# A decoder layer in split precision: another tile for the second input, sums of weight pairs issued one by one, up weights split in one piece

## The chip, the cores and the metric

One core of a Trainium2 chip. The time is that of one execution on the device in microseconds, the median of several runs. TensorE (PE) multiplies, VectorE (DVE), ScalarE (ACT) and GpSimd (POOL) do the rest, SyncE (SP) issues nearly all transfers. Each engine works through its own instructions in the order in which the program holds them.

## The reference, cut to what matters

One layer of a decoder trunk for 256 tokens of width 1024, in float32. `p` is the second input, 256 wide per token.

```python
proj = x @ w_in[i]                       # queries, keys, values of three mixers
o_a, o_b, o_c = dsa_mixer(...), dilated_mixer(...), moba_mixer(...)
gates = sigmoid(x @ w_gate[i])           # three per channel
merged = gates_0 * (o_a @ w_br_a) + gates_1 * (o_b @ w_br_b) + gates_2 * (o_c @ w_br_c)
x = layer_norm(ALPHA * x + merged @ w_out[i], ...)
h = square(relu(x @ w_up[i])) @ w_down[i]                  # 1024 -> 4096 -> 1024
ple = sigmoid(x @ w_ple_gate[i]) * (p[i] @ w_ple[i])
x = layer_norm(ALPHA * x + h + ple, ...)
```

All mixers add a bias that depends on the distance of query and key.

## The kernel before

**Split operands.** A float32 product is made of three products of rounded operands: `prod` (L180 to L189) multiplies the high and low halves as high x high, high x low and low x high. The high half of a weight is a rounded copy by ScalarE (L109 or L111), the low half the rest, a subtraction by VectorE (L118 or L122), in the first stages partly by GpSimd. The class `Weights` does that for one *unit* of 128 x 1024 weights at a time: SP loads it into one of five `raw` tiles (L102), and it is split into one of five pairs of tiles `whi` and `wlo`. `get(u)` splits up to unit u+4, so splits run some units ahead of the matmuls. The places of the unit's eight blocks of 128 columns within the tile are given by `at`. If they don't stand at one distance, `Apart.runs` cuts the work into several instructions. Up units (L639) have `UP = (16, *range(192, 1088, 128)), (64, *range(208, 1104, 128))`: the first block stands apart, so that ScalarE and VectorE each do two blocks (256 columns) and then six (768).

**Order.** The code is written in program order, and a scheduler with a timeline of its own sets each engine's order; `tc.issue_after(x)` holds an instruction until after `x` in it, `tc.keep_in_program_order` pins it.

**Stages.** First the projections, the three mixers, and between their steps the gates ("g") and merges ("c", "a"), which fill TensorE. The bias of a head lies in a tile `T` of the pool `tp`, tag "T", three buffers: `toeplitz` (L263 to L269) loads three heads' rows with three transfers (L265). The dilated mixer (`slots`, L456) keeps its exponentials in tiles `eb` of the pool `wk2`, two buffers. The second input is loaded at L582 and L583 into a tile `pr` that takes one of these two `eb` places, and is split at L584 (ScalarE) and L585 (VectorE) into `ph` and `pl`, which are used 120 us later.

Then the output product, the first norm, the gate of `p`, and the **up projection**: 32 blocks `f` of 128 features, each 8 matmuls of 512 columns with the high half of the weights (L932) and 8 of 256 with the low half (L935), then relu and square. Its tile of moving operands is `x1`.

**The down stage** multiplies the 32 blocks with rows of `w_down`. Part of them go in *pairs* (a tuple in `SEQ`, L860) by Strassen's scheme, seven products in place of eight: four units per pair, 21 matmuls, in place of two units with 12 each. A single block is one unit, 12 matmuls of 512 columns.

```python
wr[i] = r = xr[:, i % 2] if i else ...      # load(i), L880: the pair's two weight blocks
dve.tensor_tensor(t[:, 0:1024], r[:, 512:1536], r[:, 0:1024], op=ALU.subtract)      # L894
dve.tensor_tensor(r[:, 512:1024], r[:, 1024:1536], t[:, 0:512], op=ALU.subtract)    # L895
dve.tensor_tensor(t[:, 1024:1536], r[:, 1536:2048], r[:, 512:1024], op=ALU.subtract)  # L896
```

`form(i)` (L889) makes these three differences; the pair's four units are the second loaded row, the first difference, the first row after the second difference, and the third difference (512 wide). `xr` has two places. It takes the place of `x1`, so that its first loads wait for the up projection's last matmul. When the last unit of pair i is split (`last_part`), i+2 is put on the list `later`, and `weights` (L978) then calls `load(i+2)` and `form(i+2)` at once. A load waits until the splits of pair i have read the place, and VectorE's differences wait for the load. Pairs 1 and 2 are loaded and formed after the up projection (L964 to L966), pair 0 within it.

Of the kernel before, what the change touches and what calls it, by code (L numbers as in the profile page):

```python
# [11 lines left out]
F32 = mybir.dt.float32  # L12
# [130 lines left out]
def hybrid_layer(ctx: ExitStack, tc: tile.TileContext, x0, xn, pT, wqk, wva, wvb, wg, wbc, wba,  # L143
# [423 lines left out]
    for j in range(2):  # L567
# [13 lines left out]
        fill("g")  # L581
    pr = wk2.tile([128, 2, S], F32, name="pr", tag="eb")  # L582
    nc.sync.dma_start(pr, pT)  # L583
# [54 lines left out]
    u_pg = [add(wpg[i], 1024) for i in range(8)]  # L638
    UP = (16, *range(192, 1088, 128)), (64, *range(208, 1104, 128))  # L639
    u_up = [[add(wup[i], 1024, at=UP)] for i in range(32)]  # L640

# [210 lines left out]
    for b in range(2):  # L852
        for c in range(2):
# [5 lines left out]

    SEQ = ((0, 1), 2, 3, (4, 5), 6, 7, (8, 9), 10, (11, 12), 13, (14, 15), 16, (17, 18), 19,  # L860
           (20, 21), 22, 23, 24, 25)
# [27 lines left out]
    def form(i):  # L889

        t = p3.tile([128, 2, D], F32, name="rows", tag="rows") if i % 2 else Y
        wt[i] = t = t.rearrange("p b d -> p (b d)")
        r = wr[i].rearrange("p b d -> p (b d)")
        dve.tensor_tensor(t[:, 0:1024], r[:, 512:1536], r[:, 0:1024], op=ALU.subtract)  # L894
        dve.tensor_tensor(r[:, 512:1024], r[:, 1024:1536], t[:, 0:512], op=ALU.subtract)  # L895
        dve.tensor_tensor(t[:, 1024:1536], r[:, 1536:2048], r[:, 512:1024], op=ALU.subtract)  # L896

    def last_part(i):
        r = wt[i][:, 1024:1536]
        if 0 < i < len(PAIRS) - 2:  # L900
            later.append(i + 2)
        return r

    later = []
    u_dn = {}
    for k in (*SEQ, *LATE):
        if k in PAIRS:
            i = PAIRS.index(k)
            u_dn[k] = [add(f, n) for f, n in (
                (lambda i=i: wr[i][:, 1], 1024), (lambda i=i: wt[i][:, 0:1024], 1024),  # L910
                (lambda i=i: wr[i][:, 0], 1024), (lambda i=i: last_part(i), 512))]
        elif k < 30:
            u_dn[k] = [add(wdn[k], 1024)]

    def relu2(dst, ps):
# [6 lines left out]
    for f in range(32):  # L922
        if f == 16:
            with tc.issue_after(W.loads[-1]):
                load(0)
            with tc.issue_after(W.subs[-1]):
                form(0)
        ps = mmbank(512).rearrange("p (a t b) -> p a t b", a=2, b=2)
# [35 lines left out]
    for i in (1, 2):  # L964
        load(i)
        form(i)  # L966

# [9 lines left out]

    def weights(u):  # L978
        w = W.get(u)
        while later:  # L980
            i = later.pop(0)
            load(i)
            form(i)
        return w
# [191 lines left out]
```

## Time and profile before

| | |
|---|---|
| median of 3 runs | 417.64 us (417.42 to 418.87) |
| profiled execution | 417.59 us, of which 415.8 us are the span that the trace shows |
| mean granted TensorE clock | 0.996 |
| TensorE, VectorE, ScalarE, GpSimd busy | 404.6, 348.3, 277.4, 121.6 us |
| in the chain that ended last | PE 79%, DVE 9%, DMA 6% of the span |

Busy times of engines overlap, so they don't add up. A busy TensorE isn't one at full rate: matmuls are pipelined, the trace's ends of them are modelled, and the time from one start to the next tells the rate. An idle engine costs something only where TensorE waits for it, directly or through others.

### The profile page before, as it was taken

Reading aid. Unit: us, or ns where it says so; the run is one execution under the profiler, and the core shown is the slowest. Engines: PE = TensorE matmul, PEld = TensorE weight load, DVE = VectorE, ACT = ScalarE, POOL = GpSimd, SP = SyncE. Lnnn points to the kernel's source line nnn. Section 1 sums busy time; section 2 is a strip of 40 time slices with the busy share of each in tenths; the row PEclk is TensorE's granted clock in tenths of the full one; section 3 lists DMA queues with packets and bytes.
Section 4 is the critical chain, followed back from the end, with each engine's and each line's share of the span. In section 5 each row is a group of like instructions: output and inputs, shape, how many; then the busy total and the mean of one; then the engine's idle time right before and its main releaser. Section 6 shows DMA issues by size and latency. Waiting matters only on the chain.

```text
span 415.8 us, 7826 instructions
## 1 busy us (share of the span) xinstructions
PE 404.6 (97%) x2804; PEld 374.1 (90%) x2804; DVE 348.3 (84%) x650; ACT 277.4 (67%) x530; POOL 121.6 (29%) x128
## 2 busy tenths in 40 slices
PE   8999999999999999999999999999999999899993
PEld 7989999999999999999887889999999888688882
DVE  4868769897777789889978889999999797999856
ACT  5787476495798786867515668887889675558310
POOL 1579456175353657500000002433330000000001
PEclk9999999999999999999999999999999999999998
DMA  8796766567474408477981677695675377546502
GB/s 283 291 338 184 273 166 199 170 202 259 143 208 135 134 18 285 123 217 259 332 314 36 225 268 207 223 298 177 195 214 186 128 271 215 189 159 212 192 2 102
DMA packets 27964, 83.49 MB, mean 201 GB/s; under 512 B 3184, under 2 KB 6792, under 8 KB 27540
## 3 DMA queue, kind: packets, MB, share of 16 engines
q1 hardware_dynamic: 27360, 81.51, 60.3%
q10 hardware_dynamic: 468, 1.41, 0.9%
q8 instruction: 22, 0.36, 0.4%
q14 instruction: 18, 0.15, 0.1%
q0 software_dynamic: 96, 0.06, 0.0%
HBM read 81.88 MB, written 1.09 MB: 200 GB/s over the span
## 4 chain that ended last, share of the span: by engine, by line
PE 79%; DVE 9%; DMA 6%; ACT 2%; issue 2%; SPq 0%; POOL 0%; DVEq 0%; ACTq 0%
PE mm L188 34%; PE b L188 17%; PE mm L932 13%; PE mm L935 7%; DMA xr<-in_wdn_dram 3%; PE b L370 3%; DVE wlo L118 3%; PE b L522 2%; DVE wlo L122 2%; DMA G<-in_x_dram 1%; DMA pr<-in_pT_dram 1%; PE b L412 1%; ACT whi L111 1%; PE b L419 1%; DVE Y L894 1%
## 5 line engine op out<-in xcount | busy, mean ns | idle before, releaser
L111 ACT CAST whi<-raw 128x1024 fp32r<-128x1024 f32 (+3 forms) x92 | 89.5, 986 | 35.6 <-PE b L188 14.5
L122 DVE TENSOR_TENSOR wlo<-raw,whi 128x256 fp32r<-128x256 f32 (+3 forms) x118 | 94.7, 826 | 15.3 <-ACT whi L111 11.4
L188 PE MATMUL mm<-xh,whi 128*128 128x256 f32 x336 | 89.1, 278 | 0.0
L122 POOL TENSOR_TENSOR wlo<-raw,whi 128x384 fp32r<-128x384 f32 (+1 forms) x50 | 68.7, 1383 | 65.0 <-ACT whi L111 57.6
L188 PE MATMUL mm<-xl,whi 128*128 128x256 f32 x336 | 87.1, 277 | 0.0
L188 PE MATMUL mm<-xh,wlo 128*128 128x256 f32 x336 | 79.4, 278 | 0.0
L188 PEld LDWEIGHTS mm<-xh,whi 128*128 128x128 f32 x336 | 64.5, 192 | 0.9
L188 PEld LDWEIGHTS mm<-xl,whi 128*128 128x128 f32 x336 | 64.5, 192 | 0.2
L932 PE MATMUL mm<-x,whi 128*128 128x512 f32 x256 | 60.8, 380 | 0.0
L188 PEld LDWEIGHTS mm<-xh,wlo 128*128 128x128 f32 x336 | 58.7, 192 | 0.2
L188 PE MATMUL b<-whi,store 128*128 128x512 f32 x168 | 52.5, 380 | 0.3 <-DVE b L1006 0.3
L932 PEld LDWEIGHTS mm<-x,whi 128*128 128x128 f32 x256 | 46.1, 190 | 5.1
L118 DVE TENSOR_TENSOR wlo<-raw,whi 128x1024 fp32r<-128x1024 f32 (+2 forms) x38 | 43.2, 1156 | 3.5 <-ACT whi L111 3.4
L749 POOL TENSOR_TENSOR rs<-rs,half 128x1 f32<-128x1 f32 x4 | 2.7, 666 | 142.5 <-DVE rs L748 142.5
L109 ACT CAST whi<-raw 128x256 fp32r<-128x256 f32 x64 | 36.4, 613 | 6.1 <-PE b L188 3.7
L188 PEld LDWEIGHTS b<-whi,store 128*128 128x128 f32 x168 | 31.8, 189 | 4.9 <-DVE b L1006 0.7
L935 PEld LDWEIGHTS mm<-x,wlo 128*128 128x128 f32 x256 | 33.6, 191 | 1.7
L935 PE MATMUL mm<-x,wlo 128*128 128x256 f32 x256 | 33.8, 275 | 0.0
L188 PE MATMUL b<-wlo,store 128*128 128x512 f32 x84 | 32.1, 382 | 0.6 <-DVE wlo L118 0.6
L956 POOL TENSOR_TENSOR a<-a 128x128 f32<-128x128 f32 x7 | 7.3, 1042 | 57.3 <-ACT a L918 51.7
L188 PE MATMUL mm<-op,whi 128*128 128x256 f32 x128 | 22.1, 278 | 0.0
L188 PE MATMUL b<-whi,x 128*128 128x512 f32 x64 | 19.8, 384 | 0.1
(221 smaller groups left out, 818.9 us busy)
## 6 DMA issues: line engine op xcount, KB each, us to landing
raw<-in_wup_dram SPq DMA_DIRECT2D x32, 512.0 KB, 4.4
raw<-in_wg_dram SPq DMA_DIRECT2D x24, 512.0 KB, 4.6
raw<-in_wqk_dram SPq DMA_DIRECT2D x18, 512.0 KB, 5.0
raw<-in_wdn_dram SPq DMA_DIRECT2D x18, 512.0 KB, 4.3
raw<-in_wout_dram SPq DMA_DIRECT2D x8, 512.0 KB, 4.5
raw<-in_wpg_dram SPq DMA_DIRECT2D x8, 512.0 KB, 5.2
T<-tabd SPq DMA_DIRECT2D x24, 128.0 KB, 4.0
xr<-in_wdn_dram SPq DMA_DIRECT2D x6, 512.0 KB, 3.6
```

Of the source, the lines that this page charges most:

```text
L109: i = nc.scalar.copy(blocks(hi, a, b), blocks(r, a, b))
L111: i = nc.scalar.copy(hi, r)
L118: i = e.tensor_tensor(lo[:, x], r[:, x], hi[:, x].bitcast(F32), op=ALU.subtract)
L122: i = e.tensor_tensor(blocks(lo, *x), blocks(r, *x), blocks(hi, *x).bitcast(F32), op=ALU.subtract)
L188: i = pe.matmul(ps, lhsT=a[x], rhs=b[y], start=first and n == 0, stop=last and n == 2, skip_group_check=more)
L370: m = pe.matmul(ss[2 * n + h][:, QC[b]], lhsT=q[d, x, c], rhs=k[d, y, 0:128 * (b + 1)], start=i == 0, stop=i == 2)
L412: pe.transpose(t[:, 128 * i:128 * i + 128], P[:, 128 * i:128 * i + 128], ident)
L419: pe.matmul(v[:, 256 * i:].rearrange("p (m c q) -> p m c q", c=64, q=2), lhsT=V[:, i, vh], rhs=pt[:, b0:b1].rearrange("p b a (q c) -> p (b ...
L522: pe.matmul(pairs(first[f]), lhsT=w[:, k, 128 * f:128 * f + 128], rhs=inturn(x[:, k]), start=k == i == 0, stop=k == KT - 1 and i == 2)
L932: pe.matmul(ps, lhsT=hi[:, c], rhs=x1[:, :, k].rearrange("p b a t -> p a t b"), start=k == 0, stop=False)
L935: pe.matmul(ps[:, 0], lhsT=lo[:, c], rhs=x1[:, :, k, 0].rearrange("p b t -> p t b"), start=False, stop=k == KT - 1)
L956: pool.tensor_tensor(sums[2], a11, a21, op=ALU.subtract)
```

## The change

Four edits:

1. `pr` is a tile of the pool `tp`, tag "T", one of the three places of the bias tiles, no longer one of the two `eb` places.
2. `UP = 64, 80`: all eight blocks of an up unit stand in one piece, so `whi` and `wlo` are each written by one instruction of 1024 columns (L111, L118). Blocks 1 to 7 stand at the places that they had; only block 0 moves, from 16 to 64 in `whi` and from 64 to 80 in `wlo`.
3. `SEQ` has block 6 ahead of the pair (4, 5).
4. `form` is a generator: its differences come one by one. A table `steps` names for each pair i from 1 on three units, the last three of pair i-1 (for pair 1 the units of blocks 2, 3 and 6), and `weights` issues difference n of pair i after the low half of the n-th of them. `load(i+2)` stands where it stood. Pair 0 is formed as before.

```diff
-    pr = wk2.tile([128, 2, S], F32, name="pr", tag="eb")
+    pr = tp.tile([128, 3, 256], F32, name="T", tag="T")[:, 0:2]
...
-    UP = (16, *range(192, 1088, 128)), (64, *range(208, 1104, 128))
+    UP = 64, 80
...
-    SEQ = ((0, 1), 2, 3, (4, 5), 6, 7, (8, 9), 10, (11, 12), 13, (14, 15), 16, (17, 18), 19,
+    SEQ = ((0, 1), 2, 3, 6, (4, 5), 7, (8, 9), 10, (11, 12), 13, (14, 15), 16, (17, 18), 19,
...
-        dve.tensor_tensor(t[:, 0:1024], r[:, 512:1536], r[:, 0:1024], op=ALU.subtract)
+        yield dve.tensor_tensor(t[:, 0:1024], r[:, 512:1536], r[:, 0:1024], op=ALU.subtract)
...
+    for i in range(1, len(PAIRS)):
+        behind = u_dn[PAIRS[i - 1]][1:] if i > 1 else u_dn[2] + u_dn[3] + u_dn[6]
+        for n, u in enumerate(behind):
+            steps[u] = i, n
+    going = {}
...
     for i in (1, 2):
         load(i)
-        form(i)
...
     def weights(u):
+        n = W.done
         w = W.get(u)
         while later:
-            i = later.pop(0)
-            load(i)
-            form(i)
+            load(later.pop(0))
+        for n in range(n, W.done):
+            if n in steps:
+                with tc.issue_after(W.subs[n]):
+                    next(going.setdefault(steps[n][0], form(steps[n][0])))
         return w
```

How the order moves, at two places. **VectorE in the down stage**, from the split of block 10 to that of block 13. `raw` is a single block's weights, `xr` and `rows` or `Y` are the units of the pair (11, 12), L894 the first difference of the next pair, (14, 15). Before:

```order
L118 TENSOR_TENSOR wlo<-raw,whi 128x1024
L894 TENSOR_TENSOR Y<-xr 128x1024
L118 TENSOR_TENSOR wlo<-xr,whi 128x1024
L118 TENSOR_TENSOR wlo<-rows,whi 128x1024
L895 TENSOR_TENSOR xr<-xr,Y 128x512
L118 TENSOR_TENSOR wlo<-xr,whi 128x1024
L118 TENSOR_TENSOR wlo<-rows,whi 128x512
L896 TENSOR_TENSOR Y<-xr 128x512
L118 TENSOR_TENSOR wlo<-raw,whi 128x1024
```

And now, the same units (the first L896 belongs to the pair (11, 12) itself):

```order
L118 TENSOR_TENSOR wlo<-raw,whi 128x1024
L896 TENSOR_TENSOR rows<-xr 128x512
L118 TENSOR_TENSOR wlo<-xr,whi 128x1024
L118 TENSOR_TENSOR wlo<-rows,whi 128x1024
L894 TENSOR_TENSOR Y<-xr 128x1024
L118 TENSOR_TENSOR wlo<-xr,whi 128x1024
L118 TENSOR_TENSOR wlo<-rows,whi 128x512
L895 TENSOR_TENSOR xr<-xr,Y 128x512
L118 TENSOR_TENSOR wlo<-raw,whi 128x1024
```

The first difference stands behind the pair's first two splits, no longer ahead of them; the second and third each stand one or two operations later too.

**SP while the bias rows of the dilated mixer load** (`T<-tabd`), from the first of its value weights (`wvb`) on; - is before, + is now:

```order
 L102 DMA raw<-in_wvb_dram 128x768
-L265 DMA T<-tabd 128x256 x6
-L102 DMA raw<-in_wvb_dram 128x768 x3
+L265 DMA T<-tabd 128x256 x3
+L583 DMA T<-in_pT_dram 128x512
+L102 DMA raw<-in_wvb_dram 128x768
+L265 DMA T<-tabd 128x256 x2
+L102 DMA raw<-in_wvb_dram 128x768
+L265 DMA T<-tabd 128x256
+L102 DMA raw<-in_wvb_dram 128x768
```

The second input's transfer stands some 20 transfers earlier than it did, between the two bias tiles, and the later bias tile, which now takes its place, waits for L585. On ScalarE its copy moves along:

```order
L320 CAST k<-mm 128x256
L111 CAST whi<-raw 128x1024 x2
L584 CAST ph<-T 128x512
L438 ACTIVATE eb<-eb,r 128x128
L438 ACTIVATE eb<-eb,r 128x256
L332 ACTIVATE G<-mm 128x256
```

This is now; before, the same rows stood there without L584, which came some 40 instructions later. On TensorE the first transpose (L412) that reads the result of the L438 stands five matmuls (L188) later than it did.

## Rows read from the trace of the kernel before

**Rows 1.** The page, part 1: for each engine busy us, share of the span, instructions (PEld are the weight loads).

```profile
PE 404.6 (97%) x2804; PEld 374.1 (90%) x2804; DVE 348.3 (84%) x650; ACT 277.4 (67%) x530; POOL 121.6 (29%) x128
```

**Rows 2.** The chain of waits in order of time, the up projection's part: start us, us, what, and of how many instructions. L932 and L935 are its two loops of matmuls.

```profile
246.22 1.73 PE mm L932 x8
247.95 0.89 PE mm L935 x8
...
324.83 1.73 PE mm L932 x8
```

**Rows 3.** Two stretches of the down stage, TensorE alone: from and to us, length, busy us (instructions that start in it), granted clock, DMA share, GB/s.

```profile
327.40:354.40 27.00, 27.00 (x127) 1.00 0.75 246
354.40:376.10 21.70, 20.54 (x92) 1.00 0.54 173
```

**Rows 4.** TensorE's matmuls in order of time: start us, us, engine, line, operation, out<-in, rows and columns of the array, shapes, count [idle before, and what ended it]. L412 is a transpose, L419 the product with the values, L188 every product of split operands.

```profile
63.49 0.27 PE L412 MATMUL b<-ident,eb 128*128 128x128 f32 x1
...
100.06 0.27 PE L188 MATMUL mm<-xl,whi 128*128 128x256 f32 x1
100.52 0.59 PE L419 MATMUL b<-pt,V 128*128 128x512 f32 x2 [0.19 <-DVE pt L416]
...
109.74 0.28 PE L188 MATMUL mm<-xh,whi 128*128 128x256 f32 x1
110.06 0.33 PE L412 MATMUL b<-ident,e 128*128 128x128 f32 x1
...
327.50 0.38 PE L188 MATMUL b<-wlo,X 128*128 128x512 f32 x1
...
354.48 0.81 PE L188 MATMUL mm<-whi,more 128*128 128x512 f32 x3
355.89 0.48 PE L188 MATMUL b<-wlo,more 128*128 128x512 f32 x1 [0.59 <-DVE wlo L118]
...
360.16 0.38 PE L188 MATMUL b<-whi,store 128*128 128x512 f32 x1
361.10 0.48 PE L188 MATMUL b<-wlo,store 128*128 128x512 f32 x1 [0.56 <-DVE wlo L118]
```

**Rows 5.** VectorE in order of time, same columns. L118 is a split's low half, L894 and L896 are the first and third difference of a pair (L895, the second, has the third's width), L585 the second input's low half.

```profile
97.37 0.69 DVE L585 TENSOR_TENSOR pl<-pr,ph 128x512 fp32r<-128x512 f32 x1 [2.67 <-ACT ph L584]
...
318.28 1.23 DVE L118 TENSOR_TENSOR wlo<-rows,whi 128x1024 fp32r<-128x1024 f32 x1
...
332.17 1.23 DVE L894 TENSOR_TENSOR rows<-xr 128x1024 f32<-128x1024 f32 x1 [0.57 <-DMA xr<-in_wdn_dram]
...
344.37 1.23 DVE L894 TENSOR_TENSOR rows<-xr 128x1024 f32<-128x1024 f32 x1 [0.59 <-DMA xr<-in_wdn_dram]
...
349.52 0.68 DVE L118 TENSOR_TENSOR wlo<-Y,whi 128x512 fp32r<-128x512 f32 x1
350.12 0.68 DVE L896 TENSOR_TENSOR rows<-xr 128x512 f32<-128x512 f32 x1
...
353.47 1.23 DVE L894 TENSOR_TENSOR Y<-xr 128x1024 f32<-128x1024 f32 x1 [1.53 <-DMA xr<-in_wdn_dram]
354.61 1.22 DVE L118 TENSOR_TENSOR wlo<-xr,whi 128x1024 fp32r<-128x1024 f32 x1
355.75 1.22 DVE L118 TENSOR_TENSOR wlo<-rows,whi 128x1024 fp32r<-128x1024 f32 x1
```

**Rows 6.** The chain of waits in order of time, three of its transfers: start us, us from issue to landing, what.

```profile
91.05 5.64 DMA pr<-in_pT_dram
...
339.73 4.51 DMA xr<-in_wdn_dram
...
349.03 4.35 DMA xr<-in_wdn_dram
```

**Rows 7.** ScalarE in order of time, columns as in the engines' rows above. L111 is a split's high half, L438 a scaling of softmax rows, L584 the second input's high half.

```profile
59.22 1.99 ACT L111 CAST whi<-raw 128x1024 fp32r<-128x1024 f32 x2
61.12 0.80 ACT L438 ACTIVATE eb<-eb,r 128x128 f32<-128x128 f32 x2
...
96.72 0.62 ACT L584 CAST ph<-pr 128x512 fp32r<-128x512 f32 x1 [3.38 <-DMA pr<-in_pT_dram]
```

**Rows 8.** Groups of instructions, shapes apart, from 239 to 327.5 us (the up projection): line, engine, operation, out<-in, shapes, count | busy us, mean ns of one | idle just before them, and what ended it.

```profile
L122 DVE TENSOR_TENSOR wlo<-raw,whi 128x768 fp32r<-128x768 f32 x31 | 30.9, 998 | 0.5 <-ACT whi L109 0.5
L109 ACT CAST whi<-raw 128x768 fp32r<-128x768 f32 x30 | 24.8, 828 | 0.0
...
L122 DVE TENSOR_TENSOR wlo<-raw,whi 128x256 fp32r<-128x256 f32 x30 | 13.2, 440 | 1.3 <-ACT whi L109 1.3
L109 ACT CAST whi<-raw 128x256 fp32r<-128x256 f32 x29 | 11.4, 394 | 4.7 <-PE b L188 2.3 <-PE mm L932 2.2
```

**Rows 9.** The same view from 327.5 to 408 us (the down stage).

```profile
L118 DVE TENSOR_TENSOR wlo<-raw,whi 128x1024 fp32r<-128x1024 f32 x16 | 19.2, 1216 | 2.6 <-ACT whi L111 2.6
L111 ACT CAST whi<-raw 128x1024 fp32r<-128x1024 f32 x16 | 16.6, 1048 | 15.2 <-PE b L188 14.5 <-PE mm L188 0.5 <-DMA raw<-in_wdn_dram 0.3
```

**Rows 10.** SP's queue in order of time: start us, us to issue, line, what, count.

```profile
55.16 3.63 SPq L265 DMA_DIRECT2D T<-tabd  x6
```

**Rows 11.** DMA issues by line: what, queue, count, KB each, median us from issue to landing (the slowest kind).

```profile
raw<-in_wva_dram SPq DMA_DIRECT2D x4, 328.0 KB, 8.2
```

More of the change, by code (lines that the diff above doesn't have):

```diff
@@ L893, in form @@
         r = wr[i].rearrange("p b d -> p (b d)")
-        dve.tensor_tensor(t[:, 0:1024], r[:, 512:1536], r[:, 0:1024], op=ALU.subtract)
-        dve.tensor_tensor(r[:, 512:1024], r[:, 1024:1536], t[:, 0:512], op=ALU.subtract)
-        dve.tensor_tensor(t[:, 1024:1536], r[:, 1536:2048], r[:, 512:1024], op=ALU.subtract)
+        yield dve.tensor_tensor(t[:, 0:1024], r[:, 512:1536], r[:, 0:1024], op=ALU.subtract)
+        yield dve.tensor_tensor(r[:, 512:1024], r[:, 1024:1536], t[:, 0:512], op=ALU.subtract)
+        yield dve.tensor_tensor(t[:, 1024:1536], r[:, 1536:2048], r[:, 512:1024],
+                                op=ALU.subtract)
     def last_part(i):
-        r = wt[i][:, 1024:1536]
         if 0 < i < len(PAIRS) - 2:
             later.append(i + 2)
-        return r
+        return wt[i][:, 1024:1536]
     later = []
-    u_dn = {}
+    u_dn, steps = {}, {}
     for k in (*SEQ, *LATE):
@@ L926, in hybrid_layer @@
             with tc.issue_after(W.subs[-1]):
-                form(0)
+                for _ in form(0):
+                    pass
         ps = mmbank(512).rearrange("p (a t b) -> p a t b", a=2, b=2)
```

## Prediction

> **What bounds the kernel now.** I read the page first: TensorE is busy 404.6 of 415.8 us, VectorE 348.3 [rows 1]. A busy TensorE is not yet TensorE at its peak, so the next views are the stretches and the chain, which show at what rate its matmuls start. In the up projection a block is 8 matmuls of 512 columns in 1.73 us (0.216 each) and 8 of 256 in 0.89 us, 2.62 us in all, from 246.22 to the last block without a gap [rows 2]. Nothing can be gained there but by less TensorE work, and the change takes no matmul away. In the down stage the same rate holds at first: 127 matmuls in the 27.00 us up to 354.40. The next 21.70 us hold 92, where that rate gives 102 [rows 3]. Ten are missing, 10 x 0.216 = 2.2 us: that is all that TensorE loses there.
>
> Who makes it late stands in the two engines' order of time. After 354.48 three matmuls should end at 355.13, but the next starts at 355.89, released by a split (whi/wlo, the two halves of a weight) on VectorE; one more such wait, from 360.38 to 361.10, follows [rows 4]. VectorE in turn stood idle for 1.53 us at 353.47, with a pair's first difference (L894) at the head of its queue and the pair's rows still under way; the two splits that TensorE waited for, at 354.61 and 355.75, were queued behind it. Two more such idles, 0.57 and 0.59 us, are at 332.17 and 344.37 [rows 5]. The rows took 4.51 and 4.35 us from issue to landing [rows 6].
>
> A second, smaller place is near 97 us. ScalarE stood 3.38 us before L584 [rows 7] and VectorE 2.67 us before L585 [rows 5], both for the second input, whose transfer took 5.64 us [rows 6]. TensorE lost little by it: a matmul due at 100.17 starts at 100.52, and a transpose due at 109.85 starts at 110.06 [rows 4], 0.35 + 0.21 = 0.56 us, with 0.1 us for restarting.
>
> **The change, part by part.**
>
> *The differences one by one.* VectorE now meets the first difference of pair i+2 not right after the single unit behind pair i, but two splits of pair i+1 later. Between the split that frees the rows' place (and starts their load) and this difference it runs one 512-wide split, two 512-wide differences and three splits of 1024. At 0.60 and 1.14 us [rows 5] that is 3 x 0.60 + 3 x 1.14 = 5.2 us. The load needs 4.35 to 4.51 us [rows 6], so the wait goes, with 0.7 us to spare. The wait at 332.17 stays: that load starts when the up projection's last matmul has read the place that it loads into.
>
> What is late next is VectorE's own work. A pair and a single unit cost it five operations of 1.14 us (four splits, one difference) and three of 0.60: 7.5 us. TensorE needs 21 + 12 matmuls, 33 x 0.216 = 7.13 us. So VectorE loses 0.37 us of its lead in each of the four rounds that still carry differences, (8,9) to (17,18). The lead at their start, by the new order: from 332.17 seven operations of 1.14 and five of 0.60 end unit 7's split at 343.2. TensorE starts the stage at 327.28, one matmul before the row at 327.50 [rows 4], and asks for that split after two pairs, three singles and one matmul more, 79 x 0.216 later, at 344.3. The lead of 1.1 us minus 4 x 0.37 leaves about -0.4. Of the 2.2 us I therefore count **1.9 us** as gained; the bounds are 2.2 (no stall left) and 0.8 (rival 1).
>
> *Unit 6 ahead of (4,5).* The same matmuls in another order; it is in the count above. Its split now stands behind the difference at 332.17 and ends about 334.5; TensorE gets there at 327.28 + 45 x 0.216 = 337.0. Cost 0. Its cover is this 2.5 us.
>
> *Up units split whole.* Each unit loses one instruction on ScalarE and one on VectorE: 0.394 + 0.828 us become 1.048, and 0.440 + 0.998 become 1.216 [rows 8, 9], 0.17 and 0.22 us less per unit by busy time, 5.6 and 7.1 us over 32 units. TensorE waits for neither in this stage [rows 2], so the sum takes 0. The piece that was ready early was not needed early either: the first split after the up units is done at 319.5 and used at 327.50 [rows 4, 5], some 8 us of lead against a piece that is 0.8 us longer. Of eight blocks in the tile only the first changes place; seven keep the distance to each other that they have, and run at the peak now.
>
> "Perfetto Trace Analysis" of the Trainium skill (section "Optimizing Scalar/DVE Operations") gives some 60 ns for each VectorE and 93 ns for each ScalarE instruction on SBUF as overhead that grouping saves, and says that breaking instructions up can finish work sooner where an unsaturated engine leaves bubbles on others. By its figures (an estimate) 32 instructions would be worth 1.9 and 3.0 us of those engines' time, and the sum stays at 0; its second sentence is rival 3.
>
> *The second input's place.* The transfer moves from 91.05 to behind three of the six bias-row transfers that start at 55.16 and take 3.63 us to issue [rows 10]: issue at about 57.0. With the 5.64 us of its old place it lands at 62.6. What goes: the 3.38 us of ScalarE and the 2.67 of VectorE at 97, and with them the 0.56 us of TensorE, of which I take **0.5 us**; bounds 0.7 (the restarts too) and 0 (the operations queued there are late for another reason).
>
> What comes: ScalarE, in order, now meets the copy (0.62 us) right after two weight copies that end at 61.1, and behind it stand the scalings (0.80 us) for a transpose [rows 7]. Landed at 62.6, the scaling ends at 64.0. The transpose ran at 63.49 [rows 4] and now stands five matmuls of 0.11 us later, at about 64.05. So it just meets. Bounds: 0, and 2.6 us by the slowest kind of transfer in the list, 8.2 us [rows 11], which would land at 65.2; I take **0.2 us**, near the lower, since this very transfer took 5.64. SP holds the first bias row of the next stage until VectorE has read the input, about 63.6, and two value-weight loads behind it; these are first used some 15 us later, cost 0.
>
> **The sum.** 1.9 + 0.5 - 0.2 = 2.2 us. The profiled execution took 417.59 us (span 415.8 and 1.8 around it), within 0.05 of the median of 417.64. Forecast: **415.4 us**, 0.5%. What a measurement of this kernel can tell from no change is about 0.5%, 2.1 us here, so the line between faster and no change is at 415.55.
>
> **Rivals.**
> 1. *VectorE stays the bound of the down stage.* For it: 7.5 us of work against 7.13. It decides if the rows land more than 5.2 us after their issue. Half a microsecond of wait in each of four rounds adds 4 x 0.3 to 0.5; stalls of 1.4 us are then left, and the gain is 0.8 + 0.3: 416.5 us. Against it: both landings shown are under 4.6 us. 0.18.
> 2. *The early input blocks ScalarE* (the other side). In-order ScalarE waits from 61.1 until it lands; from 62.6 on each microsecond is one of TensorE at the transpose, and the copies of weights and queries behind it move with it. The gains of 2.4 us are used up at a landing 8.0 us after the issue (57.0 + 5.64 + 2.4), and the kernel is slower by over 0.5% from about 10 us: 419.8 us. Against it: 5.64 us is all that its transfer took. 0.04.
> 3. *Breaking up was what kept TensorE fed.* A whole piece is ready up to 0.8 us later than the first of two. It decides where a split leads its matmul by less than that, and the lead is some 8 us [rows 4, 5]. If the first unit of the stage is hit, 415.4 + 0.8 = 416.2. 0.02.
> 4. *The order isn't kept, or the differences wait as before:* only the input's place counts, 417.3 us. 0.04. The orders of the two programs speak against it: the difference does stand two splits later.
>
> **How the numbers follow.** The forecast's case has 0.72 and reaches from 414.6 (2.2 + 0.7 and no cost) to 416.0; by its lean to the middle I put 0.54 of it below 415.55 and 0.18 above. Rivals 1, 3 and 4 are no change, 0.24 together; all of rival 2 is counted as slower. Faster 0.54, no change 0.42, slower 0.04. The range that leaves out 2 in 10 at most: 414.4, a little under the sum of the best bounds, to 417.0, which takes in rival 1.
>
> **What would show it.** Right: no idle of VectorE for rows from 344 on; 100 or more matmuls in the 21.7 us that had 92; TensorE gapless through the up blocks at 2.62 us each, with one copy of about 1.05 and one subtraction of 1.22 us per unit; L584 near 62 us with a wait of about 1.5 us and no idle at 97. Wrong: L894 still released by its transfer; the missing matmuls at another place of the stage; the up blocks over 2.62 us; a transpose near 64 us that waits for a scaling.

## The result, and the profile after

| | before | after |
|---|---|---|
| median of the runs beside each other (6 and 6) | 417.43 us | 414.42 us (413.72 to 414.91) |
| ratio, with its 95% interval | | 0.9923 (0.9906 to 0.994) |
| profiled execution | 417.59 us | 414.56 us |
| its span | 415.8 us | 412.7 us |

The kernel became faster by 3.0 us, 0.77%. The forecast was 415.4 us, with 414.4 as the low end; 0.9923 of the 417.43 us measured beside it is 414.2 us, just under that end. Direction was right and so were most places, but the size was not: 2.2 us were counted and 3.0 came, and one wait that the change shortened, near 390 us, was not in the count. All ratios leave out four executions that took far longer than the others (424.59, 467.31, 851.14 and 2390.95 us, of the kernel before and of e_best); the medians hold them.

Both traces hold the same 2804 matmuls, so the loss can be followed by the count of matmuls: the time from the start of the 500th to that of the 800th, and so on. (They are counted from 0. 800 is near 95 us, 1000 near 117, 2400 near 324 in the up projection, 2700 near 389, 2803 is the last.) All times are us, and the last rows are experiments that come below.

```
              to 500  500-800  800-1000  1000-2400  2400-2700  2700-2803  to the end
before         59.59    35.35     22.78     206.16      65.44      19.11        7.38
after          59.67    35.52     22.06     206.17      63.19      18.91        7.24
difference     +0.08    +0.17     -0.72      +0.01      -2.25      -0.20       -0.14
counted                 +0.2      -0.5        0         -1.9        0           0

e_order        59.60    35.35     23.27     206.15      63.19      18.73        7.23
e_input        59.48    35.53     22.06     206.15      65.15      19.12        7.37
e_up           59.61    35.35     23.04     206.37      65.63      19.11        7.24
e_atonce       58.81    35.52     22.06     206.17      64.90      19.12        7.23
e_seq_old      59.84    35.54     22.06     206.27      63.19      18.98        7.24
e_pinned       58.72    35.53     22.06     206.16      63.48      18.58        7.24
e_lead256      59.76    35.55     22.06     206.18      63.32      19.98        7.25
e_lead1024     58.79    35.53     22.06     206.17      66.51      19.38        9.44
e_upold        60.70    35.52     22.06     206.16      63.19      18.73        7.24
e_lowlast      59.95    35.53     22.06     206.16      63.19      19.04        7.25
e_v4pool       60.09    35.52     22.06     206.47      63.19      18.79        7.24
e_best         59.41    35.52     22.06     206.17      63.19      18.58        7.25
```

Away from the edits one execution repeats the other within 0.02 to 0.3 us in a column. Only the first column, which holds the kernel's first loads, scatters by 1 us and more, and with it the medians. So effects of a few tenths are read from this table, one trace for each kernel, and the medians only bound them.

**The down stage.** TensorE over the same two stretches as [rows 3], in the trace of after (from, to, length, busy us and matmuls, granted clock, DMA share, GB/s):

```profile
326.90:353.90 27.00, 27.00 (x127) 1.00 0.75 256
353.90:375.60 21.70, 21.70 (x103) 1.00 0.62 196
```

The second stretch holds 103 matmuls in place of 92: nothing is missing any more. VectorE in order of time, the first differences that stood idle for their rows in [rows 5] (start us, us, line, operation, out<-in, shapes, count; an idle would stand in brackets):

```profile
332.23 1.23 DVE L894 TENSOR_TENSOR rows<-xr 128x1024 f32<-128x1024 f32 x1
...
345.49 1.23 DVE L894 TENSOR_TENSOR rows<-xr 128x1024 f32<-128x1024 f32 x1
...
352.99 1.21 DVE L894 TENSOR_TENSOR Y<-xr 128x1024 f32<-128x1024 f32 x1
```

None has an idle ahead of it. What replaced the idle shows in one row over the whole stage, of all engines (from, to, length; busy us and instructions of PE, PEld, DVE, ACT, POOL; clock, DMA share, GB/s):

```profile
332.00:390.00 58.00, 57.94 (x269) 50.43 (x268) 57.95 (x65) 35.23 (x38) 0.00 (x0) 1.00 0.67 225
```

VectorE is busy 57.95 of 58.00 us and TensorE 57.94. In the trace of before the same stretch gives 55.13 and 56.75. The two now run side by side with almost nothing to spare, and this is what the experiments turn on.

**The awaited sum near 390 us.** When the last pair is multiplied, VectorE adds up its products, between the splits of the last units. TensorE adds products of the last units onto one of these sums (`b<-b,Y`) and waits until VectorE has written it: the awaited sum. The matmul that waits is number 2702, in the table's column from 2700 on. TensorE, and the sum on VectorE, in the trace of before:

```profile
389.54 0.38 PE L188 MATMUL b<-whi,store 128*128 128x512 f32 x1
390.18 0.48 PE L188 MATMUL b<-whi,store 128*128 128x512 f32 x1 [0.26 <-DVE b L1006]
390.50 0.38 PE L188 MATMUL b<-wlo,store 128*128 128x512 f32 x1
```

```profile
389.43 0.69 DVE L1006 TENSOR_TENSOR b<-b,Y 128x512 f32<-128x512 f32 x1
```

The two steps from one start to the next are 0.64 and 0.32 us, where 0.216 each is the rate: 0.53 us are lost. In after the same place reads:

```profile
386.82 0.92 PE L188 MATMUL b<-whi,store 128*128 128x512 f32 x2
387.58 0.38 PE L188 MATMUL b<-wlo,store 128*128 128x512 f32 x1
```

```profile
386.51 0.69 DVE L1014 TENSOR_TENSOR b<-b,Y 128x512 f32<-128x512 f32 x1
```

Three starts within 0.76 us in place of 0.43: 0.32 us are still lost, though the view shows no idle there. The two columns 2400-2700 and 2700-2803 belong together, then. Their sum is 84.55 us before, 82.10 after, and 81.77 in e_best, where no step is late.

**97 us and 62 us.** ScalarE around the second input's copy (L584) in its new place, and SP's queue with the transfer (L583):

```profile
59.31 2.00 ACT L111 CAST whi<-raw 128x1024 fp32r<-128x1024 f32 x2
61.55 0.62 ACT L584 CAST ph<-T 128x512 fp32r<-128x512 f32 x1 [0.25 <-DMA T<-in_pT_dram]
62.08 0.80 ACT L438 ACTIVATE eb<-eb,r 128x128 f32<-128x128 f32 x2
```

```profile
55.24 2.72 SPq L265 DMA_DIRECT2D T<-tabd  x3
58.07 0.38 SPq L583 DMA_DIRECT2D T<-in_pT_dram  x1
```

Issued at 58.07, a microsecond later than counted, it had landed by 61.55, 3.5 us on; in its old place it took 5.64 [rows 6]. ScalarE waits 0.25 us, not the 1.5 of the forecast. At 97 us the wait of 3.38 us [rows 7] is gone:

```profile
94.94 0.37 ACT L320 CAST k<-mm 128x256 fp32r<-128x256 f32 x1 [0.78 <-PE mm L188]
95.21 1.05 ACT L111 CAST whi<-raw 128x1024 fp32r<-128x1024 f32 x1
96.28 0.59 ACT L425 COPY ov<-b 64x512 f32<-64x512 f32 x1
```

**The up projection.** Its column differs by 0.01 us, with one copy and one subtraction per unit in place of the pairs of [rows 8] (group, count | busy us, mean ns | idle before):

```profile
L111 ACT CAST whi<-raw 128x1024 fp32r<-128x1024 f32 x30 | 31.1, 1038 | 5.3 <-PE b L188 3.6 <-PE mm L938 1.6
...
L118 DVE TENSOR_TENSOR wlo<-raw,whi 128x1024 fp32r<-128x1024 f32 x30 | 37.1, 1237 | 2.2 <-ACT whi L111 2.0
```

### The profile page after: what moved, and what is told of

Read it like the earlier page. It is cut to its first block, busy times and chain, and to the rows that moved or that the text cites. A ratio compares the mean times of both kernels' runs of the same rounds, so it can differ in the third digit from the quotient of the medians.

```text
span 412.7 us, 7772 instructions
## 1 busy us (share of the span) xinstructions
PE 403.3 (98%) x2804; PEld 374.5 (91%) x2804; DVE 347.4 (84%) x618; ACT 275.1 (67%) x498; POOL 121.2 (29%) x128
## 4 chain that ended last, share of the span: by engine, by line
PE 80%; DVE 12%; DMA 4%; issue 3%; SPq 0%; ACT 0%; DVEq 0%
PE mm L188 37%; PE b L188 14%; PE mm L938 13%; PE mm L941 7%; DVE wlo L118 6%; PE b L370 3%; DMA xr<-in_wdn_dram 2%; PE b L522 2%; DMA G<-in_x_dram 1%; PE b L412 1%; PE b L419 1%; DVE wlo L122 1%; DVE Y L894 1%; DVE xr L895 1%; DVE rows L894 1%
## 5 line engine op out<-in xcount | busy, mean ns | idle before, releaser
L111 ACT CAST whi<-raw 128x1024 fp32r<-128x1024 f32 (+3 forms) x124 | 122.5, 1000 | 39.9 <-PE b L188 14.5
L188 PE MATMUL mm<-xh,whi 128*128 128x256 f32 x336 | 89.1, 278 | 0.0
L188 PE MATMUL mm<-xl,whi 128*128 128x256 f32 x336 | 87.0, 277 | 0.0
L118 DVE TENSOR_TENSOR wlo<-raw,whi 128x1024 fp32r<-128x1024 f32 (+2 forms) x70 | 82.3, 1190 | 5.4 <-ACT whi L111 5.0
L188 PE MATMUL mm<-xh,wlo 128*128 128x256 f32 x336 | 79.4, 278 | 0.0
L188 PEld LDWEIGHTS mm<-xh,whi 128*128 128x128 f32 x336 | 64.5, 192 | 0.7
L122 DVE TENSOR_TENSOR wlo<-raw,whi 128x640 fp32r<-128x640 f32 (+2 forms) x54 | 53.2, 993 | 13.6 <-ACT whi L111 12.9
L188 PEld LDWEIGHTS mm<-xl,whi 128*128 128x128 f32 x336 | 64.5, 192 | 0.2
L188 PEld LDWEIGHTS mm<-xh,wlo 128*128 128x128 f32 x336 | 58.6, 192 | 0.3
L188 PE MATMUL b<-whi,store 128*128 128x512 f32 x168 | 52.4, 380 | 0.1
L188 PEld LDWEIGHTS b<-whi,store 128*128 128x128 f32 x168 | 31.8, 189 | 4.9 <-DVE b L1014 0.5
L188 PE MATMUL b<-wlo,store 128*128 128x512 f32 x84 | 31.8, 379 | 0.0
L188 PE MATMUL mm<-op,whi 128*128 128x256 f32 x128 | 22.1, 278 | 0.0
L962 POOL TENSOR_TENSOR a<-a 128x128 f32<-128x128 f32 x7 | 3.9, 561 | 54.6 <-ACT a L923 54.6
L188 PE MATMUL b<-whi,x 128*128 128x512 f32 x64 | 19.8, 384 | 0.1
L188 PEld LDWEIGHTS mm<-op,whi 128*128 128x128 f32 x128 | 18.8, 192 | 0.3
```

The source lines that it names most:

```text
L111: i = nc.scalar.copy(hi, r)
L118: i = e.tensor_tensor(lo[:, x], r[:, x], hi[:, x].bitcast(F32), op=ALU.subtract)
L122: i = e.tensor_tensor(blocks(lo, *x), blocks(r, *x), blocks(hi, *x).bitcast(F32), op=ALU.subtract)
L188: i = pe.matmul(ps, lhsT=a[x], rhs=b[y], start=first and n == 0, stop=last and n == 2, skip_group_check=more)
```

## The experiments

In the first four the changed kernel's parts are taken one by one.

**e_order**: before, with SEQ and the differences of the change alone.

```diff
 (against the changed kernel)
-    pr = tp.tile([128, 3, 256], F32, name="T", tag="T")[:, 0:2]
+    pr = wk2.tile([128, 2, S], F32, name="pr", tag="eb")
...
-    UP = 64, 80
+    UP = (16, *range(192, 1088, 128)), (64, *range(208, 1104, 128))
```

> The kernel before with the two changes of the down stage alone: unit 6 ahead of (4,5), and the differences one by one behind the preceding pair's splits. The second input and the up units stay as before. Theory A (the order gives the whole of the down stage's gain; a unit's low half is asked for three or four matmuls after its start, so VectorE's lead stays above zero): matmul for matmul nothing moves up to 354 us, then the TensorE start offsets against before fall by 2.2 to 2.3 us by the late units and by 0.2 more at the stall near 389 us; 414.9 to 415.1 us. The recorded prediction's own step (a lead of -0.4 us at the late units): a stall of 0.3 to 0.4 stays near the late units, 415.5. Theory B (part of the gain comes from the up units' shorter work on VectorE): less than 1.7 us in the down stage, 415.7 or more.

Measured: 414.84 against 417.1 us, ratio 0.9949 (0.993 to 0.9967). The down stage's column is 63.19, the same as after: 2.25 us gone and no stall at the late units. The next column lost another 0.38. Theory A holds, theory B falls, and the prediction's own remainder of 0.3 to 0.4 us is not at the late units; 0.14 us of it are left at the awaited sum.

**e_input**: before, with the input's place alone.

```diff
-    pr = wk2.tile([128, 2, S], F32, name="pr", tag="eb")
+    pr = tp.tile([128, 3, 256], F32, name="T", tag="T")[:, 0:2]
```

> The kernel before with the second input's rows in a place of the bias tiles and nothing else. Theory A (from the two traces: matmuls 0.17 us later by 95 us, 0.72 us earlier at about 100 to 110 us, then constant): 416.8 to 416.9 us, -0.55 us. The recorded prediction: 0.5 gained and 0.2 lost, 417.1. Theory C (the 0.72 us at 100 us belongs to something else in the change): 417.4 or more.

Measured: 416.47 against 417.1 us, ratio 0.9987 (0.9968 to 1.0006), which alone tells nothing. The columns do: +0.18 and -0.72, as in after, and 22.06 in every kernel with the new place. In the old place that column is 22.78, 23.27 and 23.04. The wait for the transfer differs from one execution to the next; ScalarE in e_up and in e_order:

```profile
96.99 0.62 ACT L584 CAST ph<-pr 128x512 fp32r<-128x512 f32 x1 [3.63 <-DMA pr<-in_pT_dram]
```

```profile
97.21 0.62 ACT L584 CAST ph<-pr 128x512 fp32r<-128x512 f32 x1 [3.86 <-DMA pr<-in_pT_dram]
```

The execution that the prediction was read from had the shortest of the three waits, 3.38 us. The gain there is 0.72 to 1.21 us, mean 0.97, and the 0.17 us at 62 us come off. In this run ScalarE does not wait for the early transfer at all, and the 0.18 us are there all the same.

**e_up**: before, with the up units whole and nothing else.

```diff
-    UP = (16, *range(192, 1088, 128)), (64, *range(208, 1104, 128))
+    UP = 64, 80
```

> The kernel before with the up units split whole and nothing else. Theory A: TensorE waits for neither engine there, 0 within 0.2 us: 417.2 to 417.6, blocks of 2.62 us, and the down stage's stalls as before (the VectorE wait at its start is for a transfer and not for its own work). Theory B (VectorE's shorter work is lead that the down stage uses): its stalls shrink by 0.5 us or more, 416.9 or less. Rival 3 of the prediction (pieces kept TensorE fed): a stall of 0.3 to 0.8 us where the up units begin or where the first unit of the down stage begins, 417.8 to 418.2.

Measured: 417.26 against 417.1 us, ratio 1.0001 (0.9986 to 1.0016). Theory A by the median. The columns show 0.21 us more in the up projection and 0.19 more in the down stage. The first is scatter: of eight other traces with whole units six have 206.16 to 206.18 there, and two 206.27 and 206.47. Theory B is out, since the stalls did not shrink in sum (2.78 us against 2.77 from one start to the next). The second is taken up by e_upold.

**e_atonce**: the changed kernel with a pair's differences given with its load.

```diff
-            load(later.pop(0))
-        for n in range(n, W.done):
-            if n in steps:
-                with tc.issue_after(W.subs[n]):
-                    next(going.setdefault(steps[n][0], form(steps[n][0])))
+            i = later.pop(0)
+            load(i)
+            list(form(i))
```

> The changed kernel, but the three differences of a pair are given all at once with its load, as before; unit 6 stays ahead of (4,5), the input and the up units stay changed. Theory A (giving them behind the next pair's splits is what takes the wait for the rows off VectorE's queue): idles of VectorE for rows of 0.5 to 1.5 us come back, and 1.5 to 2.5 us of stall with them, 416.0 to 417.0 us. Theory C (unit 6's place is what gives the time): within 0.3 us of the changed kernel, 414.7.

Measured: 416.53 against 417.1 us, ratio 0.9985 (0.9971 to 0.9999), about what the input alone gives. The two columns of the down stage grow by 1.71 and 0.21 us over after. VectorE there:

```profile
341.12 1.22 DVE L118 TENSOR_TENSOR wlo<-raw,whi 128x1024 fp32r<-128x1024 f32 x1
344.00 1.23 DVE L894 TENSOR_TENSOR rows<-xr 128x1024 f32<-128x1024 f32 x1 [1.66 <-issue]
...
352.90 1.22 DVE L894 TENSOR_TENSOR Y<-xr 128x1024 f32<-128x1024 f32 x1 [0.19 <-DMA xr<-in_wdn_dram]
```

The idles are back at the same line, 1.89 us in all from the first difference to the last sums, for 1.92 us of lost TensorE time. The longer one bears no releaser in the profile; the trace has the last part of the rows landing at 343.92, 0.08 us before L894 starts. Theory C falls: with unit 6 in its new place and nothing else new in the stage, the loss stays.

**e_seq_old**: the changed kernel with unit 6 behind (4,5) again.

```diff
-    SEQ = ((0, 1), 2, 3, 6, (4, 5), 7, (8, 9), 10, ...
+    SEQ = ((0, 1), 2, 3, (4, 5), 6, 7, (8, 9), 10, ...
...
     for i in (1, 2):
         load(i)
+    list(form(1))
...
-    for i in range(1, len(PAIRS)):
-        behind = u_dn[PAIRS[i - 1]][1:] if i > 1 else u_dn[2] + u_dn[3] + u_dn[6]
+    for i in range(2, len(PAIRS)):
+        behind = u_dn[PAIRS[i - 1]][1:]
```

> The changed kernel with unit 6 back behind (4,5) (and so pair (4,5)'s own differences given at once behind the load, since two units are too few to carry three); the pairs from (8,9) on keep their differences one by one. Theory A (unit 6's place only makes room for the first pair's differences): the gain of the later rounds stays, 0 to 0.3 us of stall at (4,5), 414.4 to 414.8. Theory C (unit 6's move carries the gain): 1 us or more comes back, 415.5 or more.

Measured: 415.11 against 417.99 us, ratio 0.9927 (0.9907 to 0.9947). The down stage's column is 63.19 once more and the next 0.07 more: the move of unit 6 is worth nothing by itself, as counted.

The next three ask how close VectorE is to TensorE after the change.

**e_pinned**: the down stage's matmuls in the order of the program's text.

```diff
-            if hold and n == 0:
+            if hold and n == 0 or every:
...
-        prod(pairs(P[i]), a, b, i in fresh, end, more=True)
+        prod(pairs(P[i]), a, b, i in fresh, end, more=True, every=True)
```

> The changed kernel with the down stage's matmuls on TensorE in the order of the program text: the low half of a unit is then asked for by its second matmul, as the recorded prediction assumed, and not by its fourth or fifth as the order in the changed kernel has it. VectorE's work is the same. Theory A (the prediction's missing 0.3 us is this: the lead at unit 19 is 0.4 us in the changed kernel, 2 or 3 matmuls of 0.216 us): a stall of 0.1 to 0.4 us at unit 19 or its neighbours, each released by a split on VectorE. Theory D (VectorE is far from binding in the changed kernel): no stall in the down stage, 0 within 0.05 us in the TensorE start offsets against the changed kernel.

Measured: 414.44 against 417.99 us, ratio 0.991 (0.9886 to 0.9934). TensorE at unit 19, and the split on VectorE that it waited for:

```profile
370.99 0.59 PE L188 MATMUL b<-whi,store 128*128 128x512 f32 x2
371.60 0.48 PE L188 MATMUL b<-wlo,store 128*128 128x512 f32 x1
```

```profile
370.33 1.22 DVE L118 TENSOR_TENSOR wlo<-raw,whi 128x1024 fp32r<-128x1024 f32 x1
```

Starts of one 512-column matmul after the other are 0.216 apart. From 370.99 the low half was due at 371.42 and started at 371.60, 0.05 us after the split's end; with 0.10 us lost behind it, 0.28 us, the column's 63.48 against 63.19. It is the one stall of the stage, at the unit and for the reason that the prediction gave. But the next column falls to 18.58, the value without a stall: TensorE, late by then, comes to the awaited sum when it is done. The two columns together are 82.06 us against 82.10 in after. The text's order moves the wait from the sum to unit 19 and adds nothing to it in all. In the changed kernel the same place reads:

```profile
370.85 0.81 PE L188 MATMUL b<-whi,store 128*128 128x512 f32 x3
371.50 0.38 PE L188 MATMUL mm<-wlo,store 128*128 128x512 f32 x1
...
372.36 0.38 PE L188 MATMUL b<-wlo,store 128*128 128x512 f32 x1
372.58 0.59 PE L188 MATMUL b<-whi,store 128*128 128x512 f32 x2
373.01 0.38 PE L188 MATMUL b<-wlo,store 128*128 128x512 f32 x1
```

```profile
371.43 1.21 DVE L118 TENSOR_TENSOR wlo<-raw,whi 128x1024 fp32r<-128x1024 f32 x1
```

The three at 370.85 are unit 19's high halves for three of its four sums, run ahead of the last products of pair (17,18); the fourth is the second of the two at 372.58. Only then, at 373.01, is its first low half asked for, 0.4 us after the split's end at 372.64.

**e_lead256** and **e_lead1024**: in each of the last four rounds a part of a pair's first difference is computed twice (the same values; w is 256 or 1024).

```diff
-        yield dve.tensor_tensor(t[:, 0:1024], r[:, 512:1536], r[:, 0:1024], op=ALU.subtract)
+        yield i > 2 and dve.tensor_tensor(t[:, 0:w], r[:, 512:512 + w], r[:, 0:w], op=ALU.subtract), dve.tensor_tensor(...)
```

> The changed kernel with one more VectorE operation in each of the last four rounds of differences: the first quarter of a pair's first difference is computed twice (256 columns, by the widths beside it some 0.34 us each, 1.36 us in all). Theory A (VectorE ends the late units' splits 0.4 us ahead of TensorE): 0.9 to 1.0 us of stall in the down stage, at the units behind (14,15) to (20,21), released by splits. Theory D (not near binding): below 0.2 us.

> As the one with 256 columns, but the whole first difference is computed twice in each of the last four rounds: 1024 columns, 1.14 us each, 4.56 us in all. Theory A: 4.56 - 0.4 = 4.1 to 4.2 us of stall in the down stage, so that the two doses lie on one line of slope 1 (3.2 us apart) that meets zero at a dose of 0.4 us. Theory D: under 2 us, and the two doses on no such line.

Measured: 416.22 us, ratio 0.9961 (0.9939 to 0.9982), and 421.15 us, ratio 1.0068 (1.0042 to 1.0095). In the two columns of the stage 1.36 us of extra work cost 1.20 us, and 4.56 us cost 3.79. So VectorE's work does go almost whole into the time, and theory D is out. Two things were not as expected. The stall of the small dose is not at the late units but at the first sum that TensorE waits for near the end:

```profile
387.08 0.38 PE L188 MATMUL b<-whi,store 128*128 128x512 f32 x1
388.59 0.48 PE L188 MATMUL b<-whi,store 128*128 128x512 f32 x1 [1.13 <-DVE b L1014]
```

The backlog of splits was carried to the sums behind them. And the slope is (3.79 - 1.20) / 3.2 = 0.8, not 1. The order on VectorE tells why. In after both sums `a<-Y` stand ahead of the awaited sum (`b<-b,Y`, at 386.51):

```profile
383.04 1.28 DVE L1014 TENSOR_TENSOR a<-Y 128x512 f32<-128x512 f32 x2
```

With the large dose one of them, some 0.6 us, stands behind it:

```profile
389.45 0.69 DVE L1014 TENSOR_TENSOR b<-b,Y 128x512 f32<-128x512 f32 x1
390.05 0.68 DVE L1014 TENSOR_TENSOR a<-Y 128x512 f32<-128x512 f32 x1
```

So 3.2 - 0.6 = 2.6 us more had to be done before the sum, and 2.59 is what it cost. From the stage's first difference to the end of the awaited sum VectorE takes 54.98 us in after, 56.19 with the small dose and 58.79 with the large one: 1.21 and 3.81 us more, the cost to 0.02 us. With the large dose most of TensorE's waits are for high halves:

```profile
PE b L188 <- ACT whi L111: 1.5, 3, 0.8
PE b L188 <- DVE b L1014: 0.5, 1, 0.5
```

(waited for: us in total, times, longest). That is VectorE's work too, since ScalarE copies a difference only when VectorE has made it; the first two of these three copies:

```profile
357.40 1.05 ACT L111 CAST whi<-Y 128x1024 fp32r<-128x1024 f32 x1 [1.48 <-DVE Y L894]
...
363.15 0.62 ACT L111 CAST whi<-Y 128x512 fp32r<-128x512 f32 x1 [1.77 <-DVE Y L896]
```

TensorE's order in the stage came out differently in both kernels, and the large one's last matmuls too, which cost 2.2 us after the last matmul.

The last four try what this points to.

**e_upold**: the changed kernel with the up units in two pieces.

```diff
-    UP = 64, 80
+    UP = (16, *range(192, 1088, 128)), (64, *range(208, 1104, 128))
```

> The changed kernel with the up units split in two pieces again, as before; the input's place and the down stage's order stay changed. The recorded prediction: 0. Theory E (VectorE has no idle time left from the stage's first difference to the end, so whatever delays that first difference delays the end; with whole units it starts 8.8 us after a fixed matmul of the up projection, with pieces 8.3): the sum that TensorE waits for near 387 us comes 0.2 us earlier, and the stall there falls from 0.32 us to about 0.1: 0.2 us less by the trace.

Measured: 414.17 against 416.69 us, ratio 0.9927 (0.9906 to 0.9947), no different from the change by that. By the columns it is 0.18 us faster, all of it at the awaited sum (18.73 against 18.91), as theory E expected. The stage's first difference starts 8.16 us after the 2400th matmul, in after 8.81; in e_order, also with pieces, 8.32, and there it waits for its rows, not for VectorE:

```profile
331.68 0.42 DVE L950 TENSOR_TENSOR store<-a,store 128x256 fp32r<-128x256 f32 x1
332.69 1.22 DVE L894 TENSOR_TENSOR rows<-xr 128x1024 f32<-128x1024 f32 x1 [0.60 <-DMA xr<-in_wdn_dram]
```

With whole units VectorE comes out of the up projection too late for that. Start less idle gives the moment at which VectorE itself was ready: 7.72 us in before, e_order, e_input and e_upold alike, all with pieces, and 8.69 to 8.81 in after and seven more with whole units. So the rows set the start with pieces (8.16 to 8.54), and VectorE with whole units. The rows' landing scatters, though, and can be as late as VectorE: in after VectorE was idle for 0.02 us, so both came together, and in e_lowlast, which has whole units and another order on VectorE there, the start is at 8.76 and waits for the rows:

```profile
332.46 1.23 DVE L894 TENSOR_TENSOR rows<-xr 128x1024 f32<-128x1024 f32 x1 [0.76 <-DMA xr<-in_wdn_dram]
```

How much of the 0.18 us is such scatter one trace each can't tell.

**e_lowlast**: all high-half matmuls of a unit first, pinned.

```diff
+        for i, a, b, end in group:
+            mm(i, a[0], b[0], start=i in fresh, stop=False)
+            mm(i, a[1], b[0], start=False, stop=False)
+            fresh.discard(i)
+        for i, a, b, end in group:
+            mm(i, a[0], b[1], start=False, stop=end)
```

> The changed kernel with TensorE's order in the down stage written out: all high-half matmuls of a unit first, the low half last, up to four matmuls later than in program order. Theory A: no stall at unit 19, where program order has one of 0.28 us. Theory E (VectorE's work up to the last sums takes its 55 us whatever TensorE's order is): what TensorE doesn't wait there it waits at the awaited sum near the end, 0.2 to 0.4 us: the end of TensorE's work stays within 0.1 us of the changed kernel's. If TensorE's order alone were the limit: 0.3 us less.

Measured: 414.17 against 416.69 us, ratio 0.9934 (0.9915 to 0.9952). No stall in the stage, and 0.13 us more at the awaited sum (a stall of 0.45 there): theory E, a little past its 0.1.

**e_v4pool**: one sum on GpSimd.

```diff
-    plus(v4, v2, p5)
+    pool.tensor_tensor(v4, v2, p5, op=ALU.add)
```

> The changed kernel with one of the last sums (v4, 512 columns, 0.6 us) on GpSimd, which is idle there, and not on VectorE. Theory E: everything behind it on VectorE comes 0.6 us earlier, the awaited sum too, and the stall of 0.32 us near 387 us goes: 0.2 to 0.3 us less by the trace. Rival (GpSimd's operation slows VectorE's beside it by as much): no change or a longer stall.

Measured: 414.42 against 416.69 us, ratio 0.9938 (0.9918 to 0.9957). The column is 18.79, 0.12 less than after, but the stage's first difference had started 0.12 us earlier too, so nothing came of the moved sum. GpSimd, and VectorE beside it:

```profile
381.97 1.28 POOL L1028 TENSOR_TENSOR a<-Y 128x512 f32<-128x512 f32 x1 [73.89 <-DVE Y L1014]
```

```profile
382.46 1.87 DVE L118 TENSOR_TENSOR wlo<-raw,whi 128x1024 fp32r<-128x1024 f32 x1
```

The split that takes 1.22 us elsewhere took 1.87: 0.65 us lost for the 0.60 saved. The rival holds. The Trainium skill, "SBUF — State Buffer" (section "Who interferes with whom"), says that a VectorE instruction with two SBUF inputs, as a split is, contends with a GpSimd instruction that reads SBUF. These rows agree: the split ends 1.08 us after GpSimd's addition, about the 1.14 that it takes by itself from its start to the next.

**e_best**: the three together (the edits above).

> The changed kernel with all three: up units in two pieces, the down stage's low halves last in TensorE's order, v4 on GpSimd. Theory E: no stall at unit 19 and none at the awaited sum, 0.3 to 0.4 us less than the changed kernel by the trace; below what the medians can tell. If VectorE weren't the limit there: as the changed kernel.

Measured: 414.78 against 416.69 us, ratio 0.9939 (0.9918 to 0.996). By the columns from 2400 on it is 0.33 us faster than the changed kernel, with no stall left in the down stage or at the awaited sum; by this trace TensorE alone is the limit there. The medians can't show that: no version here is faster than the change by what this measurement can tell.

## Why the prediction was right in direction and wrong in size

- **The mechanism of the down stage: right.** The wait for rows at the head of VectorE's queue was the cause (e_order takes 2.25 us away, e_atonce brings 1.9 of it back), and no first difference is held up now. Rival 1's condition, a landing more than 5.2 us after the issue, was not met in the rounds that it is about, but nearly: in the trace of after the rows for 345.49 landed 0.06 us before, 5.06 us after the last part's issue.
- **The step that failed: "2.2 us: that is all that TensorE loses there".** The stretch in which ten matmuls were missing ends at 376.1 us. Behind it, at 390.18, TensorE waited for the sum on VectorE and lost another 0.53 us, by the same backlog. So 2.78 us were to be had (84.55 against 81.77 in e_best), 2.45 were gained, and 1.9 were counted. This term was mis-sized by 0.55 us, the largest part of the miss; the mechanism holds for it as well.
- **"The lead of 1.1 us minus 4 x 0.37 leaves about -0.4": the remainder is there, 0.32 us, but at the awaited sum and not at unit 19.** The prediction took TensorE's order from the text. In the changed kernel all four high halves of unit 19 come ahead of its first low half, three of them ahead of the pair's last products, so that the low half is asked for 0.4 us after its split and not before it. e_pinned put the text's order back: a stall of 0.28 us at unit 19, none at the sum, the same total. The size is right in part by luck. VectorE's split of unit 7 ends at 343.27, as counted, but TensorE began the stage at 326.82, not 327.28, so the lead by the text's order was 0.60 us. And the four rounds cost 0.88 us, not 1.48, since the third difference of the first one comes behind unit 10's split: from unit 7's split to unit 10's are 6.92 us, in the later rounds 7.48.

```profile
342.06 1.22 DVE L118 TENSOR_TENSOR wlo<-raw,whi 128x1024 fp32r<-128x1024 f32 x1
...
348.98 1.22 DVE L118 TENSOR_TENSOR wlo<-raw,whi 128x1024 fp32r<-128x1024 f32 x1
350.11 0.68 DVE L896 TENSOR_TENSOR rows<-xr 128x512 f32<-128x512 f32 x1
```

- **The gain at 97 us, 0.5 us: too small.** 0.72 in these two traces, 0.45 and 0.27 of it at the two matmuls that were named, and 0.72 to 1.21 over three executions of the old place. The bound of 0.7 was one execution's, and a transfer's wait is not the same in each.
- **The cost of the early place, 0.2 us: right in size** (0.17 to 0.20 in eleven traces) **and by luck.** It was counted as a late landing that holds up the transpose near 64 us. But the transfer lands 3.4 to 3.6 us after its issue, the cost is the same in e_input and e_atonce, where ScalarE doesn't wait for it, and the matmuls near 64 us are not late. The 0.17 us arise between 67 and 74 us, where the order of the matmuls differs too, without a wait that the profile shows; the cause stays open. Rival 2 had no place.
- **Unit 6: 0, right** (e_seq_old).
- **Up units whole: 0 was wrong by a little.** The up projection doesn't change, but the pieces were worth 0.18 us to the changed kernel (e_upold), as far as one trace each can tell. The cover was looked for at the first split of the stage, where 8 us of lead were named; the place that counts is the first difference, which starts some 0.5 us later with whole units. It is rival 3's kind of loss at another place.
- **Not counted at all:** 0.14 us after the last matmul, which e_up has as well as e_order. They stand before ScalarE's last multiplication, which comes 0.18 us after the GpSimd result that it waits for in before and 0.04 after it in after; why, no run tells.

Together: 0.55 (down stage and awaited sum) + 0.22 (97 us) + 0.03 + 0.14, less 0.08 by which the first 500 matmuls were later, is 0.86 us, and the span fell by 3.06 where 2.2 were counted.

## What to carry to other kernels

When an engine that works in order waits for a transfer, move the waiting operation behind work that is ready anyway. Here that gave back nearly the whole stall, and the engine's own busy time was what then limited. Compare both engines' work per round, and follow it to the last operation that both meet in (here the sums at the end): the backlog turned up there and not where it arose, and a stretch that ends before it shows only a part of the loss. Take the moment at which an operand is needed from the engine's real order of instructions; the text's order gave the wrong place for the wait here, though the same sum. Bound a wait for a transfer by several executions, as one of them may show the shortest.

## What the runs showed of the hardware that was not expected

An operation of GpSimd beside one of VectorE goes with a longer time of the latter in the softmax stage too. The second input's subtraction, 0.69 us in its old place [rows 5], took 1.49 us in its new one, where GpSimd was in an addition:

```profile
62.94 1.49 DVE L585 TENSOR_TENSOR pl<-T,ph 128x512 fp32r<-128x512 f32 x1
```

```profile
62.29 1.59 POOL L479 TENSOR_TENSOR eb<-eb 128x384 f32<-128x384 f32 x1
```

It ends 0.55 us after GpSimd's addition, as if it had waited for that end at 63.88. So it is in all eleven traces with the new place (1.49 or 1.50 us, ending 0.54 to 0.56 after GpSimd's addition), and 0.69 us in the three with the old one, where GpSimd is idle beside it; no run took the two operations apart in one place. And the same transfer of 256 KB took 3.4 to 3.6 us in one place of the program (eleven traces) and 5.6 to 6.1 in another (three).
